# Rebuilding the opening of a hybrid pooling and state-space layer: three projections together over the tiles of x

## The chip, the cores and the metric

The kernel runs on one core of one Trainium2 chip. The metric is the time of one execution on the device, in microseconds (us). All arithmetic is in 32-bit floats; the matmuls use the `float32r` form, and every operand is split into a high part `h` and a rest `l`, so that one product is made of three matmuls (`h*h`, `h*l`, `l*h`).

## The reference

One layer of a streaming encoder, for 384 tokens (256 of a new stream and 8 running streams of 16 each), with a model width of 2048:

```python
def mixer(u, ...):                       # u = rmsnorm(x, g_mix_pre)
    proj = u @ w_in                      # columns: pool 2048 | z 4096 | xBC 6144 | dt 64 | gates 4096
    a_pool, new_pool = pool_mixer(pool_in, ...)   # windows 2,4,8,16, mean minus self, per-group linear map
    ...                                  # causal conv, state-space scan, gated norm -> a_ssd
    merged = gate_A * (a_pool @ w_pool_proj) + gate_B * (a_ssd @ w_ssd_proj)
    return merged @ w_out
x = x + rmsnorm(mixer(...), g_mix_post)
x = x + rmsnorm(square(relu(rmsnorm(x, g_mlp_pre) @ w_up)) @ w_down, g_mlp_post)
```

`rmsnorm` multiplies by one over the root of the mean square of a token. `dt` is a softplus of 64 columns of `proj`, from which decays and running sums for the scan are made.

## The kernel before

Activations lie with channels on partitions: x is 16 tiles of 128 channels by 384 tokens. One projection tile (128 output columns) is 48 matmuls of 128x384: 16 channel tiles times three. Its weights come in two units of 128x1024 (512 KB): `wfetch` issues the DMA on SP's queue into one of three buffers `w`, `wsplit` makes `wh` on ScalarE (L72) and `wl` on VectorE (L74), each with three buffers, and `half` runs the 24 matmuls of a unit (L81 to L83). The gain `g_mix_pre` is folded into x when it is split (`xsplit`, L158 and L159); the norm factor `rstd` is applied after the projections, so that they do not wait for it.

The opening, in the order of the program: the constants `vec` are loaded by GpSimd's queue (the first gains are in them); GpSimd clears a tile `warm`, on which eight matmuls run; the first weight unit (in halves) and x come through SP's queue; projections p0 and p1 run over channel tiles 0 to 7 and then 8 to 15, then p2. The squares of the 16 x tiles (ScalarE, L204) are summed on VectorE (L205), summed over channels by a matmul with ones (`norm_bc`, tile `bc_x`), and the reciprocal root is found by three Newton steps over 128x384 (`rstd`). The tiles of the opening lie in pool `pha`; the next phase's pool `phc` takes their place tile by tile as they come free, and its first tile is `pst`, the pooling state, loaded by GpSimd's queue (L214).

Then come 16 pool tiles. `pool_tile(gi, k4)` reads its projection from PSUM times `rstd` (L230, L231), forms the windows (L246), and leaves the split `dh`, `dl` (L265, L266). After the first tile of group 1, 2 and 3, `pool_map` of the group before runs (tiles `pw`, 48 matmuls). `gate_a(n)` is a projection tile, a product and a sigmoid. After the last group come `gate_a(0)`, `pool_map(3)` and `dt_phase`: a projection of 128 columns, of which 64 are used, a chain of some 30 small operations on VectorE and ScalarE, and 11 transposes on TensorE (tiles `tk`, L345). Then 16 times a gate and a product with `w_pool_proj` (`pp`). A scheduler orders the instructions of each engine at build time; `behind(ins)` puts an instruction behind `ins` in its engine's order. The projections take their PSUM banks from a ring of two (`mmtile`), p0, p1, p2 and the maps from a ring of six (`sstile`).

Of the kernel before, what the change touches and what calls it, by code (L numbers as in the profile page):

```python
# [6 lines left out]
F32 = mybir.dt.float32  # L7
F32R = mybir.dt.float32r
I32 = mybir.dt.int32
# [25 lines left out]
def build(ctx, tc, io):  # L35
# [18 lines left out]
    def sstile(name):  # L54
        return pss.tile([P, 512], F32, tag="ss", name=name)
# [33 lines left out]
    def half(o, q, wl_, rhs):  # L89
        h, l = wl_  # L90
        with behind(last[0] if chain[0] else None):
            for k in range(8):
                i = q * 8 + k
                c = slice(k * P, k * P + P)
                ins = mm3(o, h[:, c], l[:, c], rhs[i][0], rhs[i][1], i == 0, i == len(rhs) - 1)
        last[0] = ins

    def proj(units, rhs, name):
        o = bank[0](f"pj_{name}")[:, :T]
        for q, src in enumerate(units):  # L100
            half(o, q, wload(src, f"{name}_{q}"), rhs)
        return o

    def norm_bc(pool, sumsq, n, name, after=None, out=None):
# [11 lines left out]
        y = pool.tile([P, T], F32, tag="nr", name=f"ny_{name}", bufs=2) if out is None else out  # L116
        v.tensor_scalar(y.bitcast(I32), hm.bitcast(I32), -0.5, MAGIC - 2.0**22 - 2.0**30, ALU.mult, ALU.add)
        for _ in range(3):
            v.tensor_tensor(a, y, y, ALU.mult)
            v.tensor_tensor(a, a, hm, ALU.mult)  # L120
            v.scalar_tensor_tensor(out=y, in0=a, scalar=1.5, in1=y, op0=ALU.add, op1=ALU.mult)
        return y
# [9 lines left out]
    win = io["w_in"]  # L132

    def in_units(i):
        return [win[i, 0], win[i, 1]]

    main = ExitStack()
    small = main.enter_context(tc.tile_pool(name="small", bufs=1, side="right"))
# [4 lines left out]
    pha = ExitStack()  # L143
    pa = pha.enter_context(tc.tile_pool(name="pha", bufs=2, reuse_waits="tile"))

    def xload(lo, hi):
        for k in range(lo, hi):
            x = pa.tile([P, T], F32, name=f"x{k}", bufs=1)
            sy.dma_start(x, io["xT"][k])
            xr.append(x)  # L150

    def xsplit(lo, hi):
        for k in range(lo, hi):
            x = xr[k]
            h = xgp.tile([P, T], F32R, name=f"xgh{k}")
            l = xgp.tile([P, T], F32R, name=f"xgl{k}")
            g1 = vec[:, V_GPRE + k : V_GPRE + k + 1]
            s.activation(h, x, AF.Copy, scale=g1)  # L158
            v.scalar_tensor_tensor(out=l, in0=x, scalar=g1, in1=h.bitcast(F32), op0=ALU.mult, op1=ALU.subtract)  # L159
            xg.append((h, l))  # L160

    gp.dma_start(vec, io["vec"])
    warm = pa.tile([P, 512], mybir.dt.bfloat16, name="warm", bufs=1)
    gp.memset(warm, 0.0)
    gp.memset(onesr.bitcast(F32), 1.0)
    wt = sstile("warm_o")
    for _ in range(NWARM):
        te.matmul(wt, warm[:, :P], warm, start=True, stop=True)
    w = wpool.tile([P, 1024], F32, tag="w", name="w_p0_0")
    h = wpool.tile([P, 1024], F32R, tag="wh", name="wh_p0_0")  # L170
    l = wpool.tile([P, 1024], F32R, tag="wl", name="wl_p0_0")
    for c in (slice(0, 512), slice(512, 1024)):
        sy.dma_start(w[:, c], win[1, 0][:, c])
        xload(len(xr), len(xr) + 4)
        s.activation(h[:, c], w[:, c], AF.Copy)
        v.tensor_tensor(l[:, c], w[:, c], h[:, c].bitcast(F32), ALU.subtract)
    w0 = h, l
    xsplit(0, 8)
    f1 = wfetch(win[2, 0], "p1_0")
    xload(8, 12)  # L180
    f2 = wfetch(win[1, 1], "p0_1")
    xload(12, 16)
    ps = sstile("pj_p0")[:, :T]
    ps1 = sstile("pj_p1")[:, :T]
    early = [ps, ps1]
    xg += [None] * 8
    half(ps, 0, w0, xg)
    half(ps1, 0, wsplit(f1), xg)
    del xg[8:]
    xsplit(8, 12)  # L190
    w2 = wsplit(f2)
    xsplit(12, 16)
    half(ps, 1, w2, xg)
    f3 = wfetch(win[2, 1], "p1_1")
    half(ps1, 1, wsplit(f3), xg)
    sy.dma_start(cst, io["cst"])
    early += [proj(in_units(1 + k), xg, f"p{k}") for k in (2,)]
    acc = pa.tile([P, T], F32, name="acc", bufs=1)
    for k in range(KD):
        if k == 0:  # L200
            s.activation(acc, xr[0], AF.Square)
        else:
            q = pa.tile([P, T], F32, tag="sq", name=f"sq{k}")
            s.activation(q, xr[k], AF.Square)  # L204
            v.tensor_tensor(acc, acc, q, ALU.add)  # L205
    norm_bc(pa, acc, DM, "x", out=rstd)
    pha.close()

    small.tile([P, 56], F32, name="pad_small")
# [2 lines left out]
    with tc.tile_pool(name="phc", bufs=1, reuse_waits="tile") as pc, tc.tile_pool(name="phc2", bufs=2, reuse_waits="tile") as pc2:  # L212
# [7 lines left out]
        A = [None] * KD  # L220
        dd = [[None] * 4 for _ in range(4)]

        def pool_tile(gi, k4):
            w = WINDOWS[gi]
            k = gi * 4 + k4
            ps = early[k] if k < 3 else proj(in_units(1 + k), xg, f"p{k}")
# [39 lines left out]
            v.tensor_tensor(l, d, h.bitcast(F32), ALU.subtract)  # L266
            dd[gi][k4] = (h, l)

        def pool_map(gi):
            for hf in range(2):  # L270
                h, l = wload(io["pool_w"][gi, hf], f"pw{gi}_{hf}")
                for n2 in range(2):
                    n = gi * 4 + hf * 2 + n2
                    o = sstile(f"pw{n}")[:, :T]
                    for k in range(4):
                        c = slice((n2 * 4 + k) * P, (n2 * 4 + k + 1) * P)
                        mm3(o, h[:, c], l[:, c], dd[gi][k][0], dd[gi][k][1], k == 0, k == 3)
                    ah = pc.tile([P, T], F32R, name=f"ah{n}")
                    al = pc.tile([P, T], F32R, name=f"al{n}")
# [5 lines left out]
                    A[n] = (ah, al)  # L285

        def gate_a(n):
            ps = proj(in_units(17 + n), xg, f"ga{n}")
# [4 lines left out]
            return sg  # L293

        def dt_phase(pb):
            ps = proj(in_units(0), xg, "dt")
            n64 = lambda nm: pb.tile([NH, T], F32, name=nm)
            dtb = vec[:NH, V_DTB : V_DTB + 1]
            alog = vec[:NH, V_ALOG : V_ALOG + 1]
            nA = pb.tile([NH, 1], F32, name="nA")  # L300
            s.activation(nA, alog, AF.Exp)
            raw, ab, e, t1, t2, q = (n64(x) for x in ("raw", "ab", "e", "t1", "t2", "q"))
            v.tensor_tensor(raw, ps[:NH], rstd[:NH], ALU.mult)
# [34 lines left out]
            sy.dma_start(decb, dec_scr.partition_broadcast(P))  # L338
            srcs = [cum[:, i * P : i * P + P] for i in range(3)] + [dt[:, i * P : i * P + P] for i in range(3)]
            srcs += [dtw[:, i * P : i * P + P] for i in range(3)] + [nb[:, :P], nb[:, TP:]]  # L340
            for r in range(2):
                part = srcs[r * 8 : r * 8 + 8]
                o = sstile(f"tk{r}")
                for i, a in enumerate(part):
                    te.transpose(o[:, i * NH : i * NH + NH], a, ident[:NH, :NH])  # L345
# [714 lines left out]
```

## Time and profile before

| | us |
|---|---|
| median of 3 runs | 2846.51 (2845.68 to 2846.81) |
| profiled execution, its own time | 2847.36 |
| span of its instructions | 2845.6 |
| TensorE busy in the span | 2818.9 |
| VectorE busy | 1574.4 |
| ScalarE busy | 1096.4 |

The profiled execution's own time is 1.8 us more than its span, which runs from its first to its last instruction. Engines: PE is TensorE (PEld its weight loads), DVE VectorE, ACT ScalarE, POOL GpSimd, SP SyncE; a q behind the name is the engine's queue of instructions. A row of the windows view gives a stretch of the span, its length, the busy time of each engine with its count of instructions, the granted clock of PE, the share of time in which the 16 DMA engines are busy, and GB/s. A row of the timeline gives start, duration, engine, line, operation, tiles and shape, and in brackets the idle time before it and what ended it.

### The profile page before, as it was taken

The page shows a single profiled execution, that of the slowest core. Times are in us where ns is not written, and L with a number is a line of the kernel's source. Part 1 is how long each engine was busy: PE and PEld are TensorE (multiplying, and loading weights), DVE is VectorE, ACT ScalarE, POOL GpSimd, SP SyncE. Part 2 cuts the span into 40 slices and gives each one's busy share as a digit, 9 for nine tenths or more (in the row PEclk, how much of TensorE's full clock was granted, in tenths as well). Part 3 has the DMA queues.
Part 4 walks back from the last instruction along what each step waited for, and adds up shares of the span by engine and source line. Part 5 has one row for each costly group of instructions (what it writes and reads, how often), then busy time and mean ns, then how long its engine had stood idle before and what let it go on. Part 6 is the DMA issues. An engine that isn't in the chain of part 4 may idle for free.

```text
span 2845.6 us, 39445 instructions
## 1 busy us (share of the span) xinstructions
PE 2818.9 (99%) x15823; PEld 2676.3 (94%) x15823; DVE 1574.4 (55%) x2251; ACT 1096.4 (39%) x1592; POOL 97.0 (3%) x156
## 2 busy tenths in 40 slices
PE   8999999999999999999999999999999999999998
PEld 7999999999999999999999987989898998989897
DVE  7674334786887887886533334534444444444445
ACT  5343224444544544444422234533232333333233
POOL 0000000000100100001000000000000000000000
PEclk9999999999999999999999999999999999999999
DMA  5444445556655655656644453333434343343433
GB/s 203 133 133 142 137 137 196 173 184 213 201 181 205 201 181 202 208 199 215 200 154 149 147 181 119 126 127 126 132 126 126 129 131 126 127 130 129 126 127 125
DMA packets 141655, 448.77 MB, mean 158 GB/s; under 512 B 17201, under 2 KB 40817, under 8 KB 136865
## 3 DMA queue, kind: packets, MB, share of 16 engines
q1 hardware_dynamic: 133152, 410.14, 44.5%
q0 software_dynamic: 8320, 36.13, 3.5%
q8 instruction: 124, 2.03, 0.3%
q14 instruction: 59, 0.48, 0.1%
HBM read 404.48 MB, written 41.72 MB: 157 GB/s over the span
## 4 chain that ended last, share of the span: by engine, by line
PE 96%; DVE 2%; ACT 1%; DMA 1%; issue 0%; SPq 0%; DVEq 0%; ACTq 0%
PE pj_up L83 6%; PE pj_up L81 6%; PE pj_up L82 6%; PE wd L775 6%; PE wd L776 6%; PE wd L774 6%; PE pj_x L81 5%; PE pj_x L83 5%; PE pj_x L82 5%; PE pj_sp L82 3%; PE pj_z L81 3%; PE pj_z L82 3%; PE pj_sp L83 3%; PE pj_z L83 3%; PE pj_sp L81 3%; PE pj_pp L83 2%
## 5 line engine op out<-in xcount | busy, mean ns | idle before, releaser
L83 PE MATMUL pj_up<-x1h,wl_up 128*128 128x384 f32 x1024 | 343.1, 335 | 0.4 <-DVE wl_up L74 0.4
L82 PE MATMUL pj_up<-x1l,wh_up 128*128 128x384 f32 x1024 | 343.0, 335 | 0.0
L81 PE MATMUL pj_up<-x1h,wh_up 128*128 128x384 f32 x1024 | 342.9, 335 | 0.0
L74 DVE TENSOR_TENSOR wl_wd<-w_wd,wh_wd 128x1024 fp32r<-128x1024 f32 x127 | 155.6, 1225 | 261.9 <-ACT wh_wd L72 261.9
L775 PE MATMUL wd<-wl_wd,hh 128*128 128x512 f32 x762 | 296.7, 389 | 0.0
L776 PE MATMUL wd<-wh_wd,hl 128*128 128x512 f32 x762 | 296.6, 389 | 0.0
L774 PE MATMUL wd<-wh_wd,hh 128*128 128x512 f32 x762 | 296.2, 389 | 0.0
L72 ACT ACTIVATE wh_wd<-w_wd 128x1024 fp32r<-128x1024 f32 x127 | 134.8, 1061 | 350.7 <-PE wd L776 284.1
L74 DVE TENSOR_TENSOR wl_up<-w_up,wh_up 128x1024 fp32r<-128x1024 f32 x128 | 156.8, 1225 | 199.6 <-ACT wh_up L72 199.6
L72 ACT ACTIVATE wh_up<-w_up 128x1024 fp32r<-128x1024 f32 x128 | 135.8, 1062 | 326.5 <-PE pj_up L82 265.8
L81 PE MATMUL pj_x<-xgh,wh_x 128*128 128x384 f32 x768 | 257.4, 335 | 0.0
L82 PE MATMUL pj_x<-xgl,wh_x 128*128 128x384 f32 x768 | 256.6, 334 | 0.0
L83 PE MATMUL pj_x<-xgh,wl_x 128*128 128x384 f32 x768 | 256.6, 334 | 0.0
L83 PEld LDWEIGHTS pj_up<-x1h,wl_up 128*128 128x128 f32 x1024 | 192.5, 188 | 0.9 <-DVE wl_up L74 0.7
L81 PEld LDWEIGHTS pj_up<-x1h,wh_up 128*128 128x128 f32 x1024 | 192.5, 188 | 0.5
L82 PEld LDWEIGHTS pj_up<-x1l,wh_up 128*128 128x128 f32 x1024 | 192.7, 188 | 0.3
L81 PE MATMUL pj_z<-xgh,wh_z 128*128 128x384 f32 x512 | 171.1, 334 | 0.0
L83 PE MATMUL pj_z<-xgh,wl_z 128*128 128x384 f32 x512 | 171.1, 334 | 0.0
L775 PEld LDWEIGHTS wd<-wl_wd,hh 128*128 128x128 f32 x762 | 143.0, 188 | 29.8 <-DVE wl_wd L74 0.3
L82 PE MATMUL pj_z<-xgl,wh_z 128*128 128x384 f32 x512 | 171.0, 334 | 0.0
L81 PE MATMUL pj_sp<-abh,wh_sp 128*128 128x384 f32 x512 | 171.0, 334 | 0.0
L82 PE MATMUL pj_sp<-abl,wh_sp 128*128 128x384 f32 x512 | 171.0, 334 | 0.0
(292 smaller groups left out, 6089.0 us busy)
## 6 DMA issues: line engine op xcount, KB each, us to landing
w_up<-w_up SPq DMA_DIRECT2D x128, 512.0 KB, 3.4
w_wd<-w_down SPq DMA_DIRECT2D x128, 512.0 KB, 3.4
w_x<-w_in SPq DMA_DIRECT2D x96, 512.0 KB, 4.4
w_z<-w_in SPq DMA_DIRECT2D x64, 512.0 KB, 3.5
w_sp<-w_ssd SPq DMA_DIRECT2D x64, 512.0 KB, 3.5
w_ga<-w_in SPq DMA_DIRECT2D x32, 512.0 KB, 3.4
w_pp<-w_pp SPq DMA_DIRECT2D x32, 512.0 KB, 3.4
hs<-ssm SPq DMA_DIRECT2D x16, 1024.0 KB, 6.4
```

Source lines behind the costliest of these rows:

```text
L72: s.activation(h, w, AF.Copy)
L74: v.tensor_tensor(l, w, h.bitcast(F32), ALU.subtract)
L81: te.matmul(out, wh, xh, start=first, stop=False)
L82: te.matmul(out, wh, xl, start=False, stop=False)
L83: return te.matmul(out, wl, xh, start=False, stop=last)
L774: te.matmul(o[b], mh, wh[:, c], start=k == 0, stop=False)
L775: te.matmul(o[b], mh, wl[:, c], start=False, stop=False)
L776: te.matmul(o[b], ml, wh[:, c], start=False, stop=k == nk - 1)
```

## The change

- The three projections p0, p1 and p2 run together over the channel tiles of x: for each tile k, one strip `w_e[k]` of 128x384 weights, and 9 matmuls. From k = 2 on, strips come in pairs of one DMA of 384 KB.
- All loads of the opening are on SP's queue, in the order of use: x0 with the 16 gains in front of it (`x0g`), strip 0, x1, strip 1, then two x tiles and a pair of strips in turn. `vec` comes last, by the same queue.
- The squares come from x with tokens on partitions (three tiles of 128x2048, 1 MB each, loaded in between), one ScalarE instruction per tile with a running sum; Newton's steps run on 128x3. Three scaled identities, split in two, and two matmuls with ones bring the result into `rstd`.
- p3 belongs to the opening too, in the two-bank ring, ahead of the norm's matmuls.
- `gate_a(0)` moves from before `pool_map(3)` to before `pool_map(0)`, and each `pool_map` in the loop is put behind the last projection on TensorE.
- `dt_phase` comes ahead of `pool_map(3)`. Its 64 columns of high and of low weights are packed side by side into one 128-column operand: two matmuls per channel tile, 32 in all, where there were 48; the upper half is copied down and added. The 11 transposes move behind the gate loop's fourth round (`dt_turn`).

```diff
-    gp.dma_start(vec, io["vec"])
     warm = pa.tile([P, 512], mybir.dt.bfloat16, name="warm", bufs=1)
...
-    for c in (slice(0, 512), slice(512, 1024)):
-        sy.dma_start(w[:, c], win[1, 0][:, c])
-        xload(len(xr), len(xr) + 4)
...
+    x0 = pa.tile([P, KD + T], F32, name="x0g", bufs=1)
+    sy.dma_start(x0, io["x0g"])
...
+    def eload(k, n):
+        w = wpool.tile([P, 1024], F32, tag="w", name=f"w_e{k}")[:, : n * T]
+        sy.dma_start(w.rearrange("p (k n) -> p k n", k=n), io["w_e"][k : k + n].rearrange("k p n -> p k n"))
...
+    eload(0, 1)
+    xload(1)
+    eload(1, 1)
+    for k in range(2, KD, 2):
+        xload(k)
+        xload(k + 1)
+        eload(k, 2)
+        if k in (6, 10):
+            tload(len(xs3))
+    f0 = wfetch(in_units(4)[0], "p3_0")
+    sy.dma_start(ident, io["cst"][:, C_IDENT : C_IDENT + P])
+    tload(2)
+    f1 = wfetch(in_units(4)[1], "p3_1")
+    sy.dma_start(cst[:, P:], io["cst"][:, P:])
+    sy.dma_start(vec, io["vec"])
...
+    for k in range(2, KD, 2):
+        xsplit(k)
+        xsplit(k + 1)
+        hl = esplit(k)
+        eprod(k, 0, hl)
+        eprod(k + 1, 1, hl)
+        if k in (10, 14):
+            square((k - 10) // 4, turn[0])
+    ps3 = mmtile("pj_p3")[:, :T]
+    half(ps3, 0, wsplit(f0), xg)
+    square(2, None)
+    half(ps3, 1, wsplit(f1), xg)
...
+    newton(yx, ax, hx)
+    for b in range(3):
+        y1 = yx[:, b : b + 1]
+        v.tensor_scalar(dgh[:, b, :], ident, y1, None, ALU.mult)
...
+    te.matmul(bc, onesr, dgh.rearrange("p b t -> p (b t)"), start=True, stop=False)
+    te.matmul(bc, onesr, dgl.rearrange("p b t -> p (b t)"), start=False, stop=True)
+    s.copy(rstd, bc)
...
-            ps = proj(in_units(0), xg, "dt")
+            ps = mmtile("pj_dt")[:, :T]
+            for q in range(2):
...
+                for k in range(8):
+                    c = hl[:, k].rearrange("p a n -> p (a n)")
+                    te.matmul(ps, c, xg[q * 8 + k][0], start=q + k == 0, stop=False)
+                    te.matmul(ps, c, xg[q * 8 + k][1], start=False, stop=q * 8 + k == KD - 1)
...
+            with behind(s.copy(raw, ps[NH:])):
+                s.activation(nA, alog, AF.Exp)
+            v.tensor_tensor(raw, ps[:NH], raw, ALU.add)
...
                 if gi and k4 == 0:
-                    pool_map(gi - 1)
-        sg = gate_a(0)
+                    if gi == 1:
+                        sg = gate_a(0)
+                    pool_map(gi - 1, last[0])
+        srcs = dt_phase(pc)
         pool_map(3)
-        dt_phase(pc)
...
+            if n == 3:
+                dt_turn(srcs)
```

More of the change, by code (lines that the diff above doesn't have):

```diff
@@ L102, in proj, with newton, norm_bc @@
         return o
-    def norm_bc(pool, sumsq, n, name, after=None, out=None):
+    def newton(y, a, hm):
+        v.tensor_scalar(y.bitcast(I32), hm.bitcast(I32), -0.5, MAGIC - 2.0**22 - 2.0**30, ALU.mult, ALU.add)
+        for _ in range(3):
+            v.tensor_tensor(a, y, y, ALU.mult)
+            v.tensor_tensor(a, a, hm, ALU.mult)
+            v.scalar_tensor_tensor(out=y, in0=a, scalar=1.5, in1=y, op0=ALU.add, op1=ALU.mult)
+        return y
+    def norm_bc(pool, sumsq, n, name, after=None):
         h = pool.tile([P, T], F32R, tag="nr", name=f"nh_{name}", bufs=2)
@@ L115, in norm_bc @@
         a = pool.tile([P, T], F32, tag="nr", name=f"na_{name}", bufs=2)
[L116 to L122, printed above, removed]
+        y = pool.tile([P, T], F32, tag="nr", name=f"ny_{name}", bufs=2)
+        return newton(y, a, hm)
     a_scr = [dram.tile([P, T], F32, name=f"a_scr{i}") for i in range(32)]
@@ L200, in build, with esplit @@
+    early = [sstile(f"pj_p{n}")[:, :T] for n in range(3)]
+    turn = [None]
+    def esplit(k):
+        w, n = eu[k]
+        h = wpool.tile([P, 1024], F32R, tag="wh", name=f"wh_e{k}")[:, : n * T]
+        l = wpool.tile([P, 1024], F32R, tag="wl", name=f"wl_e{k}")[:, : n * T]
         if k == 0:
-            s.activation(acc, xr[0], AF.Square)
+            v.tensor_copy(h, w)
         else:
-            q = pa.tile([P, T], F32, tag="sq", name=f"sq{k}")
-            s.activation(q, xr[k], AF.Square)
@@ L205, in build, with eprod @@
-            v.tensor_tensor(acc, acc, q, ALU.add)
-    norm_bc(pa, acc, DM, "x", out=rstd)
+            turn[0] = s.activation(h, w, AF.Copy)
+        v.tensor_tensor(l, w, h.bitcast(F32), ALU.subtract)
+        return h, l
+    def eprod(k, j, hl):
+        h, l = hl
+        col = lambda n: slice(j * T + n * P, j * T + n * P + P)
+        xh, xl = xg[k]
+        if k == 0:
+            for a, b in ((h, xh), (h, xl), (l, xh)):
+                for n in range(3):
+                    te.matmul(early[n], a[:, col(n)], b, start=a is h and b is xh, stop=False)
+            return
+        for n in range(3):
+            last[0] = mm3(early[n], h[:, col(n)], l[:, col(n)], xh, xl, False, k == KD - 1)
@@ new lines, in build, with square @@
+    sx, hx, ax, yx = (pa.tile([P, 3], F32, name=f"{n}x", bufs=1) for n in ("s", "h", "a", "y"))
+    def square(b, ins):
+        with behind(ins):
+            s.activation(xs3[b], xs3[b], AF.Square, accum_out=sx[:, b : b + 1])
+    for k in (0, 1):
+        hl = esplit(k) if k == 0 else None
+        xsplit(k)
+        eprod(k, 0, hl or esplit(k))
+    for k in range(2, KD, 2):
+        xsplit(k)
+        xsplit(k + 1)
[4 more added lines that the diff above has]
+            square((k - 10) // 4, turn[0])
@@ L219, in build @@
             bufs.append(b)
-        A = [None] * KD
+        A = [
+            (pc.tile([P, T], F32R, name=f"ah{n}"), pc.tile([P, T], F32R, name=f"al{n}")) for n in range(KD)
+        ]
         dd = [[None] * 4 for _ in range(4)]
@@ L267, in pool_tile, with pool_map @@
             dd[gi][k4] = (h, l)
-        def pool_map(gi):
+        def pool_map(gi, after=None):
             for hf in range(2):
@@ L274, in pool_map @@
                     o = sstile(f"pw{n}")[:, :T]
[L275 to L279, printed above, removed]
+                    with behind(after):
+                        for k in range(4):
+                            c = slice((n2 * 4 + k) * P, (n2 * 4 + k + 1) * P)
+                            mm3(o, h[:, c], l[:, c], dd[gi][k][0], dd[gi][k][1], k == 0, k == 3)
+                    ah, al = A[n]
                     sc = vec[:, V_PSC + n : V_PSC + n + 1]
@@ L987 @@
     w_in = a["w_in"][0]
[L988 removed]
+    cols = [i * P for i in range(3, 16)] + [12352 + i * P for i in range(32)]
     for g in range(G):
```

91 lines of the change are left out of this document (42 added, 49 removed).

## The prediction

> **What bounds the kernel now.** I read the page first, then the windows of 20 us, then TensorE's waits, then the timeline around each hole.
>
> ```profile
> span 2845.6 us, 39445 instructions
> ...
> PE 2818.9 (99%) x15823; PEld 2676.3 (94%) x15823; DVE 1574.4 (55%) x2251; ACT 1096.4 (39%) x1592; POOL 97.0 (3%) x156
> ```
>
> ```profile
> 0.00:20.00 20.00, 14.76 (x63) 10.14 (x64) 12.69 (x21) 15.04 (x27) 1.56 (x7) 1.00 0.92 332
> 20.00:40.00 20.00, 19.31 (x110) 18.76 (x109) 16.48 (x26) 11.11 (x18) 0.77 (x3) 1.00 0.65 213
> 40.00:60.00 20.00, 14.79 (x76) 14.31 (x75) 17.50 (x43) 8.12 (x22) 2.16 (x4) 0.83 0.29 94
> 60.00:80.00 20.00, 20.00 (x118) 20.00 (x117) 12.42 (x21) 9.05 (x16) 1.08 (x2) 1.00 0.42 135
> ```
>
> TensorE is busy for 99% of the span, so elsewhere only fewer matmuls can help. The opening is different: a full stretch holds 118 matmuls, the first three hold 63 (8 of them warm-ups), 110 and 76. The first hole is an early one, the second lies in 40 to 60:
>
> ```profile
> PE pw L81 <- ACT dh L265: 5.2, 1, 5.2
> ...
> PE tk L345 <- DVE cum L319: 0.5, 1, 0.5
> ```
>
> ```profile
> 46.00:48.00 2.00, 0.00 (x0) 0.00 (x0) 2.00 (x6) 1.64 (x8) 0.85 (x2) 0.90 0.39 160
> 48.00:54.00 6.00, 3.19 (x10) 3.03 (x11) 5.94 (x21) 2.62 (x9) 0.77 (x2) 0.50 0.42 125
> 54.00:56.00 2.00, 2.00 (x12) 2.00 (x11) 1.97 (x8) 1.10 (x3) 0.54 (x1) 0.89 0.10 35
> ```
>
> The first pooling map waits 5.2 us for the first pool tiles (VectorE is at 2.00 of 2.00 meanwhile), and that idleness halves the granted clock until about 54.4.
>
> **How much the opening loses.** I count lost time as the time on the clock less the matmuls done at full pitch.
>
> ```profile
> 45.66 0.42 DVE L230 TENSOR_TENSOR pbuf<-pj_p,rstd 128x256 f32<-128x256 f32 x1
> ...
> 50.04 0.17 DVE L262 TENSOR_TENSOR d<-d,pbuf 128x16 f32<-128x16 f32 x1
> ...
> 53.11 0.28 DVE L231 TENSOR_TENSOR pbuf<-pj_p,rstd 128x128 f32<-128x128 f32 x1
> ...
> 77.74 0.42 DVE L230 TENSOR_TENSOR pbuf<-pj_p,rstd 128x256 f32<-128x256 f32 x1 [1.97 <-PE pj_p L83]
> ...
> 86.06 0.42 DVE L230 TENSOR_TENSOR pbuf<-pj_p,rstd 128x256 f32<-128x256 f32 x1 [1.50 <-PE pj_p L83]
> ```
>
> The last two rows are the ends of p5 and p6: 8.32 us for 48 matmuls, a pitch of 0.1733 us. At 77.74 TensorE has done six projections (288), one pooling map (48) and the norm's 2: 338 matmuls, 58.6 us. So 19.1 us are lost by then. The second hole is 5.2 us of waiting and about 1.8 us at half clock (some 3.6 us after the map starts), 7.0 together; 12.1 us are lost ahead of it.
>
> **Part A, the new opening (the large term).** Its start:
>
> ```profile
> 1.26 0.69 POOL L162 DMA_DIRECT2D vec<-vec  x1 [0.82 <-POOLq L1038]
> 1.95 0.54 POOL L164 MEMSET warm<- 128x512 bf16 x1
> ...
> 2.55 3.60 PE L168 MATMUL warm_o<-warm 128*128 128x512 bf16 x8 [2.55 <-POOL warm L164]
> ...
> 6.14 1.63 ACT L158 ACTIVATE xgh<-x,vec 128x384 fp32r<-128x384 f32 x3 [1.98 <-DMA vec<-vec]
> ...
> 6.81 0.45 PE L81 MATMUL pj_p<-xgh,wh_p 128*128 128x384 f32 x1 [0.66 <-ACT xgh L158]
> ```
>
> The first real matmul (6.81) waits for x times its gain, and that for `vec` (6.14). With the gains in x0 this wait goes. What is late next is the warm-up: the memset moves up by the 0.69 us of `vec`'s issue, so the warm matmuls end at about 2.55 + 3.60 - 0.69 = 5.5. I take 5.5 plus 0.4 for matmuls still at a cold clock: 5.9.
>
> Then 144 matmuls, 25.0 us: without stalls the three projections end at 30.9. Splits don't bound it: a pair of channel tiles costs ScalarE two x splits (0.54 each from the row above) and 3/4 of a weight split, VectorE much the same:
>
> ```profile
> L72 ACT ACTIVATE wh_wd<-w_wd 128x1024 fp32r<-128x1024 f32 x127 | 134.8, 1061 | 350.7 <-PE wd L776 284.1 <-PE pj_up L82 66.6
> L74 DVE TENSOR_TENSOR wl_up<-w_up,wh_up 128x1024 fp32r<-128x1024 f32 x128 | 156.8, 1225 | 199.6 <-ACT wh_up L72 199.6
> ```
>
> That is 1.9 us on ScalarE and about 2.0 on VectorE, against 3.1 us of matmuls. The token-major squares add two of about 2.1 us (twice the 1061 ns) to ScalarE; the three-deep rings take those up. The supply may bound it:
>
> ```profile
> 2.00:6.00 4.00, 3.45 (x8) 1.04 (x8) 0.69 (x1) 0.65 (x2) 0.63 (x2) 1.00 0.97 291
> 6.00:12.00 6.00, 4.27 (x20) 3.03 (x19) 4.51 (x9) 5.13 (x11) 0.00 (x0) 1.00 1.01 375
> 12.00:20.00 8.00, 7.03 (x38) 6.07 (x37) 7.48 (x12) 8.00 (x16) 0.00 (x0) 1.00 1.01 397
> 20.00:28.00 8.00, 8.00 (x48) 8.00 (x47) 6.95 (x12) 5.87 (x10) 0.77 (x3) 1.00 0.82 270
> ```
>
> Up to the last pair of strips come 16 x tiles and 16 strips of 192 KB and two token tiles of 1 MB: 8.4 MB. And one load comes that nobody moved:
>
> ```profile
> 20.25 0.54 POOL L214 DMA_DIRECT2D pst<-state_pool  x1 [17.62 <-DMA w_p<-w_in]
> ```
>
> `pst` (0.98 MB) takes the place of the pool's first tiles, up to x4 by their sizes, and was held until x4 had been squared. Now x4's last reader is its split, at about 10 us, so `pst` lands in the middle of the stream: 9.4 MB. At the rates of these rows (291, then 375, then 385 between the last full two) that ends at 2 + 4 + 6 + 15.5 = 27.5. Behind it come the last split, 1.7 us, and the last 18 matmuls, 3.1 us, of which 0.3 can start ahead: 32.0. At 291 GB/s throughout it would be 2 + 32.2 + 4.5 = 38.7; with `pst` outside, 30.9. I take 32.0, nearest to the rows with a full queue: 32.0 - 25.0 = 7.0 us lost, between 5.5 (no stall and no cold matmul) and 13.7.
>
> The Trainium skill bears on this stream ("DMA: Bandwidth & Descriptors", "Rules for kernel authors"): it wants 1 MiB or more per DMA for full bandwidth. The loads here are mostly 192 and 384 KB; the 375 GB/s of 6 to 12, when x tiles of 192 KB were among the loads, speak against a large loss.
>
> Next, p3 runs 8.3 us, to 40.7 with two matmuls of the norm behind it. The norm is ready by then: the third token tile lands some 4 us after the last strips (1.6 MB), its square takes 2.1, eleven operations on 128x3 and six on 128x128 some 4 (0.17 and 0.28 us each, by the rows at 50.04 and 53.11), about 38. Cover left: 2 to 3 us. From 40.7 p4 and `gate_a(0)` give 16.6 us of work ahead of the first map, while the four pool tiles need about 11; so the 5.2 us wait and its half clock go. What is late next is the bank: `gate_a(0)` is the second user after p3 of the two-bank ring, and needs pool tile 3 to have read p3. The rows at 45.66 and 53.11 put that read 7.7 us after the first; with `rstd` at about 41.6 it is done at 49.4, when p4 ends at 49.2. I take 0.4 us, between 0 and 2.
>
> Gain of part A: 19.1 - 7.0 - 0.4 = 11.7 us (between 3.4 and 13.6).
>
> **Part B, dt.** 16 matmuls fewer: 16 x 0.1733 = 2.8 us off TensorE, certain. The moved transposes take with them the 0.5 us wait quoted above. Added: a wait at `pool_map(3)`, which had a gate and now has dt's 32 matmuls as cover.
>
> ```profile
> 177.59 0.42 DVE L230 TENSOR_TENSOR pbuf<-pj_p,rstd 128x256 f32<-128x256 f32 x1 [0.66 <-PE pj_p L83]
> ...
> 184.69 0.56 DVE L266 TENSOR_TENSOR dl<-d,dh 128x384 fp32r<-128x384 f32 x1 [0.59 <-ACT dh L265]
> ```
>
> The last pool tile takes 7.7 us from its projection's end to `dl`. Cover: 32 + 9 matmuls, 7.1 us. That leaves 0.5; the copy of dt's upper half and an exponential may stand ahead of `dh` on ScalarE, so I take 1.0 (0 to 2). All of TensorE's later work is queued behind it. dt's VectorE chain now runs under the map and pp0, and the map's last results have pp0's first 45 matmuls as cover (7.8 us); I cost that at nothing, 1 us if the chain holds them up. Part B: 2.8 + 0.5 - 1.0 = 2.3 us.
>
> **Sum.** 11.7 + 2.3 = 14.0 us off the profiled execution's 2847.36: 2833.4. The median shown is 0.85 lower, so 2832.5. The extra 3 MB of token loads lie in a stage counted above.
>
> **Rivals.**
> 1. *Supply-bound opening.* Short transfers and `pst` hold the stream at 291 GB/s: 13.7 us lost, part A gives 5.0 and the whole 7.3: 2839. For it: the rate of 2 to 6, when 192 KB tiles were the bulk. Against: the next six us.
> 2. *The hole only moves.* The pool tiles still end last at the maps or at `gate_a(0)`'s bank, and about 7 us come back with the halved clock: 2839.5. Against: 16.6 us of cover over 11.
> 3. *Slower: the stream starves.* SP's queue works in order; if it waits for a `w` buffer, x and tokens behind wait too, and the engines run dry between short loads. It costs all of the gain when the 9.4 MB come at below 236 GB/s, and is slower by over 0.2% below about 206 GB/s: at 200 the last strips land at 49, the projections end at 53.5, 28.5 us are lost, and the time is 2854. For it: 20 to 28, when the queue did wait for buffers, ran at 270. Against: the ring of three pairs is refilled well ahead of 3.1 us per pair.
>
> By the skill's rule the third is the one to fear: that page's table has 138 GB/s for a transfer of 64 KB and 341 for 1 MB; no run here shows those. A second rule, "TensorE: Matmul & The Clock Gate", Part 1, says that an idle window of 3.4 us throttles the clock; the trace has it after some 2 us (idle from about 45.6, clock at 0.90 in 46 to 48). By the trace a stall of 2 us in the stream could already add 1.8 us; the range has it.
>
> **How the numbers follow.** Forecast 0.66, rival 1 0.14, rival 2 0.08, rival 3 0.06; 0.06 for smaller losses together that bring it within 0.2% (5.7 us, about what a measurement of this kernel can tell). The upper end 2839.5 takes in rivals 1 and 2; the lower 2829.5 is no stall at all: 13.6 + 2.8 + 0.5 = 16.9. Faster 0.88, same 0.06, slower 0.06.
>
> **What would show it.** First real matmul near 5.5; the three projections' end near 32; no wait of `pw` for `dh`; no 0.50 clock at 48 to 54; `pst` issued near 10 us; `pj_dt` with 32 matmuls; a short wait of `pw` behind dt. DMA rates below 300 GB/s between 6 and 27, or a wait of several us at `pj_ga`, would prove me wrong.

## The result, and the profile after

The changed kernel takes 2836.1 us (median of 6 runs, 2834.49 to 2838.28), the kernel before 2846.66 beside it (6 runs, 2845.68 to 2847.43): 10.6 us or 0.37% less, a ratio of 0.9963 [0.995, 0.9976]. 2832.5 was forecast, within 2829.5 to 2839.5. The profiled execution of the changed kernel took 2834.49, with a span of 2832.7: 12.9 less than the span before.

The head of its page, then TensorE's waits in the first 700 us (what waited for what: us in total, times, longest), then the windows of 20 us:

```profile
span 2832.7 us, 39399 instructions
...
PE 2812.7 (99%) x15807; PEld 2673.1 (94%) x15807; DVE 1562.9 (55%) x2245; ACT 1092.0 (39%) x1582; POOL 96.6 (3%) x155
```

```profile
PE pj_ga L81 <- DVE pbuf L291: 3.5, 1, 3.5
PE warm_o L154 <- POOL warm L150: 1.3, 1, 1.3
PE pj_p L81 <- ACT wh_e L212: 0.4, 1, 0.4
```

```profile
0.00:20.00 20.00, 18.28 (x86) 15.41 (x87) 11.61 (x19) 12.38 (x20) 0.87 (x6) 1.00 0.92 335
20.00:40.00 20.00, 20.00 (x117) 20.00 (x116) 12.76 (x29) 13.84 (x17) 0.84 (x3) 1.00 0.92 367
40.00:60.00 20.00, 16.55 (x96) 16.26 (x95) 17.16 (x45) 9.51 (x26) 2.72 (x5) 1.00 0.49 150
60.00:80.00 20.00, 20.00 (x118) 20.00 (x117) 10.77 (x15) 10.16 (x15) 0.54 (x1) 1.00 0.40 132
```

TensorE's matmuls in the first three stretches rise from 63, 110 and 76 to 86, 117 and 96. The waits of `pw` and of `tk` are gone, and 40 to 60 is at full clock. One hole is left: `gate_a(0)` waits 3.5 us for VectorE to read pool tile 3 out of its bank. The timeline around it, of TensorE, VectorE and ScalarE in turn:

```profile
52.14 0.41 PE L81 MATMUL pj_ga<-xgh,wh_ga 128*128 128x384 f32 x1 [3.45 <-DVE pbuf L291]
```

```profile
40.90 0.42 DVE L290 TENSOR_TENSOR pbuf<-pj_p,rstd 128x256 f32<-128x256 f32 x1 [0.36 <-ACT rstd L264]
...
41.97 1.21 DVE L74 TENSOR_TENSOR wl_ga<-w_ga,wh_ga 128x1024 fp32r<-128x1024 f32 x1
45.53 1.23 DVE L74 TENSOR_TENSOR wl_ga<-w_ga,wh_ga 128x1024 fp32r<-128x1024 f32 x1 [2.35 <-ACT wh_ga L72]
46.67 1.30 DVE L306 TENSOR_TENSOR win<-pbuf 128x518 f32<-128x518 f32 x2
...
51.71 0.28 DVE L291 TENSOR_TENSOR pbuf<-pj_p,rstd 128x128 f32<-128x128 f32 x1
```

```profile
42.12 0.30 ACT L300 COPY pstg<-pbuf 128x120 f32<-128x120 f32 x1
44.44 1.06 ACT L72 ACTIVATE wh_ga<-w_ga 128x1024 fp32r<-128x1024 f32 x1 [2.01 <-PE pj_p L82]
45.40 0.47 ACT L297 COPY pbuf<-pst 128x120 f32<-128x120 f32 x2
...
48.55 1.06 ACT L72 ACTIVATE wh_pw<-w_pw 128x1024 fp32r<-128x1024 f32 x1 [0.25 <-PE pj_p L82]
```

The pool tiles start at 40.9 (41.6 was forecast), and tile 3's read ends at 52.0, 11.1 us after, not 7.7. In the middle both engines stand still. ScalarE has the second weight split of `gate_a(0)` next in its order, and that waits 2.0 us for a `wh` buffer, which p4's matmuls hold. Behind it stand two small copies from `pst` (L297) which the pool tiles need; VectorE waits 2.35 us at its own half of the same split, with the window sums (L306) behind it.

The first matmul of the next large phase (`pj_x`) marks the end of everything that the change touches: it starts at 462.23 before and at 450.14 after, 12.1 us earlier. I use that time below. The remaining 0.8 of the two spans lies behind it, where the two programs do the same work.

### The profile page after: what moved, and what is told of

It reads as the page before. It is cut to its first block, busy times and chain, and to the rows that moved or that the text cites. A ratio compares the mean times of both kernels' runs of the same rounds, so it can differ in the third digit from the quotient of the medians.

```text
span 2832.7 us, 39399 instructions
## 1 busy us (share of the span) xinstructions
PE 2812.7 (99%) x15807; PEld 2673.1 (94%) x15807; DVE 1562.9 (55%) x2245; ACT 1092.0 (39%) x1582; POOL 96.6 (3%) x155
## 4 chain that ended last, share of the span: by engine, by line
PE 98%; DVE 1%; ACT 0%; DMA 0%; issue 0%; SPq 0%; DVEq 0%; ACTq 0%
PE pj_up L83 6%; PE pj_up L81 6%; PE pj_up L82 6%; PE wd L853 6%; PE wd L854 6%; PE wd L852 6%; PE pj_x L81 5%; PE pj_x L83 5%; PE pj_x L82 5%; PE pj_sp L82 3%; PE pj_z L81 3%; PE pj_z L82 3%; PE pj_sp L83 3%; PE pj_z L83 3%; PE pj_sp L81 3%; PE pj_ga L81 2%
## 5 line engine op out<-in xcount | busy, mean ns | idle before, releaser
L854 PEld LDWEIGHTS wd<-wh_wd,hl 128*128 128x128 f32 x762 | 143.0, 188 | 29.7
```

Of the source, the lines that this page charges most:

```text
L854: te.matmul(o[b], ml, wh[:, c], start=False, stop=k == nk - 1)
```

## The experiments

"The opening's mark" is the start of that first `pj_x` matmul in the profiled execution. The kernel before ran beside all of them, at medians of 2846.55 to 2846.74.

**1. The changed kernel again**, as the base for the others.

> The changed kernel itself, on the same chip as the next three. Theory (clock gate): its spread comes from the 3.5 us hole ahead of gate_a(0), which is as long as the gate's window of 3.4 us and costs a stretch of half clock in some executions and none in others; so some executions lie near 2834.5 and others 1.5 to 4 us above, and the profiled one has either no 0.50 stretch near 50 us (time near 2834.5) or one (near 2836 to 2838). Rival (chip noise): the spread is of every kernel here, and kernels without the hole show it too.

Median 2837.16 (5 runs, 2835.14 to 2838.86), ratio 0.9967 [0.9954, 0.9979]. The profiled execution has the same hole of 3.5 us, but a span of 2836.3 and the mark at 453.04, 2.9 later. The windows of 2 us, first of the changed kernel's first profile and then of this one, tell why (the columns are those of the other windows; the granted clock is the third number from the end):

```profile
50.00:52.00 2.00, 0.00 (x0) 0.00 (x0) 2.00 (x6) 0.94 (x6) 0.54 (x1) 1.00 0.00 0
52.00:54.00 2.00, 1.86 (x11) 1.89 (x12) 2.00 (x6) 1.06 (x4) 0.54 (x1) 1.00 0.20 69
```

```profile
50.00:52.00 2.00, 0.00 (x0) 0.00 (x0) 2.00 (x6) 0.94 (x6) 0.54 (x1) 0.89 0.01 2
52.00:54.00 2.00, 1.79 (x6) 1.82 (x7) 2.00 (x7) 1.06 (x4) 0.54 (x1) 0.50 0.19 67
```

The same hole was followed by a halved clock (until 58.4) in one execution and not in the other. So a hole of this length has two prices, 3.5 us and about 6.4; the difference is of the size of this kernel's scatter, 3.7 us. The granted clock over each run goes the same way: 0.998 in the fastest of the five (2835.14), 0.996 in the two slowest (2838.12 and 2838.86). The rival holds in part: the kernel before scatters by 2.5 us, and the next kernel, which lacks the hole, by 2.3.

**2. p3 in the ring of six**, so that `gate_a(0)` needs no bank that p3 holds.

```diff
-    ps3 = mmtile("pj_p3")[:, :T]
+    ps3 = sstile("pj_p3")[:, :T]
```

> p3 takes its PSUM bank from the ring of six instead of the ring of two, so gate_a(0) need not wait for pool tile 3 to read it. Theory (the hole is the bank): the 3.5 us wait of pj_ga goes to 0 to 0.3, nothing else on TensorE waits for it because the first map needs dl of tile 3 only 18 us after p4's start; span 3.5 us shorter than the changed kernel's 2832.7, near 2829.2, median near 2831, and all runs within 1 us of each other since no hole over 2 us is left. Rival (the hole moves): the pool tiles still end last and pw waits 2 to 4 us for dl; time within 1 us of the changed kernel. Rival (noise): median falls by 3.5 but the spread of 4 us stays.

Median 2831.46 (5 runs, 2830.39 to 2832.68), ratio 0.9947 [0.9933, 0.9961]. No wait is left behind the opening; TensorE's waits and two of the windows:

```profile
PE pj_p L81 <- ACT wh_e L212: 1.4, 1, 1.4
PE warm_o L154 <- POOL warm L150: 1.3, 1, 1.3
```

```profile
40.00:60.00 20.00, 20.00 (x117) 20.00 (x116) 17.24 (x41) 10.92 (x28) 2.71 (x5) 1.00 0.48 161
60.00:80.00 20.00, 20.00 (x117) 20.00 (x116) 12.77 (x25) 10.23 (x16) 0.54 (x1) 1.00 0.44 149
```

The mark is at 447.05, 3.1 earlier than the best of the changed kernel (the hole's 3.5, less 1.0 more at the start, where the wait for a strip differs from run to run; the 0.6 left I did not place). This kernel (kernel 2 below) has the lowest median of all: 5.7 us below the changed kernel on the same chip, and none of its runs reaches into that one's. The runs were to lie within 1 us of each other; they spread over 2.3, all at a granted clock of 0.998, so part of the scatter has another cause, which stays open.

**3. One split moved behind the pool tiles.** If the waiting split causes the hole, its place in the order should matter. The second split of `gate_a(0)` goes behind tile 3's read and copy (`read3`, on VectorE and ScalarE; `hold` puts the next split behind them); the bank stays in the ring of two.

```diff
+                hold[:] = read3
+                half(ps, 1, wload(u[1], "ga0_1"), xg)
+                hold[:] = [None, None]
```

> The bank stays in the ring of two; only the order changes: the split of gate_a(0)'s second weight unit (wh on ScalarE, wl on VectorE) is put behind pool tile 3's read of p3. Theory (queue order): in the changed kernel ScalarE's copies of the pooling state stand behind that wh, which waits 2.0 us for a weight buffer, and VectorE's window sums behind both; with the split behind, tile 3 reads p3 at about 48.5 instead of 52.0, the wait of pj_ga falls from 3.5 to about 0.4 us, and the time is within 1 us of the kernel with six banks. Rival (VectorE is simply full): the reads come no earlier than 51, the wait stays at 3 us or more, or turns into a wait of pj_ga for its second unit.

Median 2835.45 (5 runs, 2834.85 to 2836.53), ratio 0.9961 [0.9949, 0.9974]. The expectation missed: 2.9 us of the hole stayed. The three engines again (the first row names a small operation on `d`, which stands next to tile 3's read; the read, L292, ends at 52.35, 0.15 us before the matmul, as in the changed kernel):

```profile
52.50 0.47 PE L81 MATMUL pj_ga<-xgh,wh_ga 128*128 128x384 f32 x1 [2.89 <-DVE d L325]
```

```profile
46.76 0.41 DVE L291 TENSOR_TENSOR pbuf<-pj_p,rstd 128x256 f32<-128x256 f32 x1
...
50.97 0.56 DVE L329 TENSOR_TENSOR dl<-d,dh 128x384 fp32r<-128x384 f32 x1 [2.10 <-ACT dh L328]
...
52.07 0.28 DVE L292 TENSOR_TENSOR pbuf<-pj_p,rstd 128x128 f32<-128x128 f32 x1
```

```profile
49.47 1.06 ACT L72 ACTIVATE wh_pw<-w_pw 128x1024 fp32r<-128x1024 f32 x1 [2.26 <-PE pj_p L82]
50.43 0.51 ACT L328 ACTIVATE dh<-d 128x384 fp32r<-128x384 f32 x1
```

Tile 2 was read 2.5 us earlier (46.76 against 49.22). Then the next split in the order, `wh_pw` of the map, took the place of the first: it waits 2.26 us for a buffer, `dh` stands behind it, `dl` waits for `dh`, and tile 3's read stands behind `dl`.

**4. Both splits behind.** As 3, and the map's first split behind the last `dh` of group 0 (`split[3]`) as well.

```diff
+                if gi == 0 and hf == 0:
+                    hold[:] = [split[3], read3[1]]
                 h, l = wload(io["pool_w"][gi, hf], f"pw{gi}_{hf}")
+                hold[:] = [None, None]
```

> As the kernel with the gate's second split behind pool tile 3's read, and the first pooling map's weight split (wh_pw, which stood next in ScalarE's queue and waited 2.3 us there for a buffer) behind the last dh of group 0 as well; the bank stays in the ring of two. Theory (ScalarE's queue: a weight split that waits for a buffer holds up the small copies and dh behind it, and VectorE behind those): tile 3 reads p3 near 50.3 instead of 52.1, the wait of pj_ga falls from 2.9 to 1.0 to 1.5 us. Rival (VectorE's own work is what is late): the read stays at 51.5 or later and the wait at 2.5 us or more.

Median 2832.95 (4 runs, 2832.25 to 2833.69), ratio 0.9954 [0.9937, 0.997]; the mark is at 447.83, and the clock stays full. Tile 3's read ends at 49.7.

```profile
PE pj_ga L81 <- DVE d L325: 1.0, 1, 1.0
```

With the bank still in the ring of two, the order of two splits alone cuts the hole from 3.5 to 1.0. So the cause has two halves, either of which can be taken away: a bank that must be read first, and a reader that stands behind waiting splits.

**5. The order alone, without the new opening.** The kernel before, with `gate_a(0)` ahead of the first map, the maps behind the last projection, dt ahead of `pool_map(3)` and the transposes later.

```diff
-                    pool_map(gi - 1)
-        sg = gate_a(0)
+                    if gi == 1:
+                        sg = gate_a(0)
+                    pool_map(gi - 1, last[0])
+        srcs = dt_phase(pc)
         pool_map(3)
-        dt_phase(pc)
```

> The kernel before, with its old opening and its 48 matmuls for dt, and only the order changed: gate_a(0) before pool_map(0), maps behind the last projection, dt ahead of pool_map(3), transposes behind the fourth round of the gate loop. Theory (the second hole is a matter of order): of the 7.0 us of the hole at 46 to 54 most goes; p3's bank is read at about 53.4, when p4 ends, so the wait is under 1 us, the 0.5 us of tk goes too: 6.5 to 7.5 us faster than before, near 2839.5. Theory (the rebuild of the loads does the work): under 3 us faster, with a hole of 3 us or more at pj_ga.

Median 2847.35 (11 runs, 2846.54 to 2850.64), ratio 1.0004 [0.9995, 1.0013]: nothing gained. The hole went to a place that I had not named, the start of p4. In the windows of 2 us before it TensorE does nothing, and the clock halves:

```profile
PE pj_p L81 <- DVE pbuf L231: 6.2, 1, 6.2
```

```profile
46.00:48.00 2.00, 0.00 (x0) 0.00 (x0) 2.00 (x4) 1.28 (x8) 1.08 (x2) 1.00 0.21 77
48.00:50.00 2.00, 0.00 (x0) 0.00 (x0) 2.00 (x9) 0.72 (x3) 0.00 (x0) 0.55 0.62 148
50.00:52.00 2.00, 0.58 (x2) 0.61 (x3) 1.94 (x8) 1.41 (x5) 0.00 (x0) 0.50 0.45 160
```

I had missed that p2 too has its bank in the ring of two: the description of the kernel before puts it into the ring of six, and that is wrong (only p0, p1 and the maps are there). p4 needs p2's bank, and p2 is read only once the norm is there. In the kernel before, the same bank was taken until the second row here ends, at 51.64:

```profile
50.81 1.01 PE L81 MATMUL pw<-dh,wh_pw 128*128 128x384 f32 x2 [5.21 <-ACT dh L265]
```

```profile
51.36 0.28 DVE L231 TENSOR_TENSOR pbuf<-pj_p,rstd 128x128 f32<-128x128 f32 x1
```

Three of the map's matmuls stood ahead of p4 in TensorE's order, and p4 began right behind them, at 51.94. So the old hole had two causes that ended within 1 us of each other, `dh` for the map and p2's bank for p4, and taking away the first alone gains nothing.

**6. The order and the banks, without the new opening.** As 5, with p2 and p3 both made early and in the ring of six.

```diff
+    bank[0] = sstile
+    early += [proj(in_units(1 + k), xg, f"p{k}") for k in (2, 3)]
+    bank[0] = mmtile
```

> The kernel before with its old opening, its loads, its norm and its 48 matmuls for dt; the new order (gate_a(0) ahead of pool_map(0), dt ahead of pool_map(3), transposes late), and p2 and p3 in the ring of six, since with order alone the 6.2 us wait stood at p4 for p2's bank. Theory (the second hole is order and banks, the opening's rebuild isn't needed for it): no wait over 1 us between 40 and 70, the 7.0 us of the hole and 0.5 of tk go; the first matmul of pj_x starts near 455 instead of 462.2, and the time is near 2839.5. Rival (the norm has to come earlier too): a wait of 3 us or more at pj_p, pj_ga or pw stays, and the time is above 2843.

Median 2840.72 (10 runs, 2839.51 to 2841.28), ratio 0.9979 [0.997, 0.9988]; the mark is at 456.35. About 2839.5 and a mark near 455 were expected, with no wait over 1 us. With banks to go with it, the order alone brings 5.9 us at the mark, half of what the whole change did, at full clock and with a rest of 1.4 us before the first map:

```profile
PE pw L81 <- ACT dh L267: 1.4, 1, 1.4
```

**7. dt with 48 matmuls again**, on kernel 2.

```diff
-            ps = mmtile("pj_dt")[:, :T]
...
+            ps = proj([io["w_in"][125, 0], io["w_in"][125, 1]], xg, "dt")
```

> The changed kernel with p3 in the ring of six (no hole left at the gate), and dt's projection as before: 48 matmuls with the full unit pair of 128 columns in place of the packed 32. Theory (TensorE's count is all that counts there): 16 x 0.1733 = 2.8 us slower than the six-bank kernel's 2831.5, near 2834.2, and the first matmul of pj_x 2.8 us later than its 447.05 (less or more by the early stall, which was 1.4 us in that profile). Rival (hidden, or the packing costs as much as it saves in the chain behind it): within 1 us of the six-bank kernel.

Median 2833.32 (4 runs, 2833.04 to 2833.67), ratio 0.9954 [0.9939, 0.9969]. The mark is at 449.83, 2.8 after kernel 2's, which fits the 16 matmuls of the packing; but TensorE's early waits for strips differ between the two profiles (0.9 here, 1.4 there), so the 2.8 is good to about half a us. The median moved by only 1.9, on another chip.

**8. The norm from channel-major x**, on kernel 2: `norm_x` makes 16 squares and their sum, splits it, runs two matmuls with ones between the halves of p3, and takes Newton's steps on 128x384; no token loads.

```diff
-        if k in (6, 10):
-            tload(len(xs3))
...
+    norm_x()
     half(ps3, 1, wsplit(f1), xg)
```

> The changed kernel with p3 in the ring of six, and the norm as before: squares of the 16 channel tiles, summed on VectorE, two matmuls between the halves of p3, Newton's steps on 128x384; no token-major loads (3 MB less in the opening's stream). Theory A (the token-major norm carries part of the gain): rstd is ready near 44.5 instead of 41, the pool tiles end 3 to 4 us later, pw or pj_ga waits 2 to 3 us, and the time is 2 to 4 us above the six-bank kernel's 2831.5. Theory B (p4 and the gate give cover enough, the norm's form is worth nothing): within 1 us of it, or a little faster since the early stall for the strips goes with the 3 MB.

Median 2835.79 (4 runs, 2832.37 to 2837.12), ratio 0.9961 [0.9946, 0.9976]. The profiled execution was the fastest of these, with the mark at 447.69 and a wait of 0.7 us at `bc_x`, in the middle of p3; it does not explain the others. A second profile of the same kernel:

> The kernel with the channel-major norm and p3 in the ring of six once more, for a second profile: its first profile had no wait over 0.7 us in the opening and a time near 2832.4, while its other executions lay between 2835.7 and 2837.1. Theory (a late rstd leaves the pool tiles so little room that a slightly later stream opens a wait at pw): this profile shows a wait of pw or pj_p of 1 us or more between 40 and 70 us, or a 0.50 stretch of the clock there, and a time above 2834. Rival (the difference lies elsewhere): no wait over 1 us before 450 us, and the loss shows further on, or the time is near 2832.4 again.

This execution took 2835.82, with the mark at 450.63. The first matmul of the norm, and two windows behind it:

```profile
37.48 0.41 PE L255 MATMUL bc_x<-nh_x,onesr 128*128 128x384 f32 x1 [1.85 <-ACT nh_x L252]
```

```profile
38.00:40.00 2.00, 2.00 (x10) 2.00 (x11) 1.55 (x2) 0.28 (x1) 0.00 (x0) 0.82 0.58 234
40.00:42.00 2.00, 2.00 (x8) 2.00 (x7) 1.90 (x5) 0.00 (x0) 0.00 (x0) 0.50 0.35 63
```

The sum of squares from channels comes later than TensorE wants it, by 0.7 us in one execution and 1.85 in the other, and the longer wait also brought a halved clock. Neither theory had this place: the wait stands at the norm's own matmul, and no wait of `pw` or `pj_ga` follows. Over the runs the granted clock is 0.998 in the fast one and 0.997 in the other three and in the second profile. The kernel with the token-major norm is about 4 us faster in the median (2835.79 against 2831.46, on two chips); what was run against it is the old norm with its matmuls inside p3, and the old norm with them behind p3 was not run. Two profiles are not enough to explain every run.

**9. `pst` early**, on kernel 2: `x0g` is allocated behind the other x tiles, so that it no longer lies where `pst` goes.

```diff
+    xt_ = {k: pa.tile([P, T], F32, name=f"x{k}", bufs=1) for k in range(1, KD)}
     x0 = pa.tile([P, KD + T], F32, name="x0g", bufs=1)
```

> The changed kernel with p3 in the ring of six, and one change of layout: x0 with the gains lies behind x15 in the opening's pool, so that pst (0.98 MB, GpSimd's queue) takes the place of x1 to x5 and can go out once x5 is split, near 11 us, instead of 27.3 us, where the last read of the gains held it. This is the state that the prediction assumed. Theory (the stream has slack for it): the strips land 2.5 us later, TensorE waits 0 to 0.5 us more, the time is within 0.5 us of the six-bank kernel's 2831.5. Theory of the prediction (supply binds): the three projections end 1 to 2 us later, pj_p waits for wh_e or xgl between 15 and 30 us, the time is 1 to 2 us longer.

GpSimd's issue of `pst`, first in the changed kernel and then here, and TensorE's waits here:

```profile
27.33 0.68 POOL L272 DMA_DIRECT2D pst<-state_pool  x1 [25.92 <-DMA cst<-cst]
```

```profile
12.15 0.68 POOL L273 DMA_DIRECT2D pst<-state_pool  x1 [10.75 <-DMA w_e<-w_e]
```

```profile
PE pj_p L81 <- ACT wh_e L213: 3.5, 4, 1.5
```

Median 2834.05 (4 runs, 2832.56 to 2834.99), ratio 0.9956 [0.9942, 0.9969], and the mark at 449.79, 2.7 us later than kernel 2's. With 0.98 MB more in the stream, strips come late: behind `pst` TensorE waits 1.27 us until 20.46 and 1.54 until 28.54, where kernel 2 has no wait (its 1.4 ends at 10.08).

**10. Strips 2 and 3 as loads of their own**, on kernel 2, since the first pair is what TensorE waits for at 10 us.

```diff
-    for k in range(2, KD, 2):
+    for k in (2, 3):
+        xload(k)
+        eload(k, 1)
+    for k in range(4, KD, 2):
```

> The six-bank kernel, and strips 2 and 3 as loads of their own behind their x tiles, in place of one pair; the only wait left in its opening is TensorE's for the split of that first pair (0.4 us in one profile, 1.4 in another). Theory (the first pair comes late because it waits for its second half and a 768-wide split): that wait goes, 0.4 to 1.2 us off the six-bank kernel's 2831.5, near 2830.7. Rival (the stream itself is late there): the wait moves to the next strip and the time stays within 0.3 us.

Median 2832.83 (5 runs, 2831.05 to 2833.94), ratio 0.9952 [0.9938, 0.9965], the mark at 448.22; not better. The waits now stand at the following strips:

```profile
PE pj_p L81 <- ACT wh_e L215: 1.5, 3, 0.8
...
PE pj_p L83 <- DVE wl_e L216: 0.4, 1, 0.4
```

**11. The new opening with `gate_a(0)` at its old place**, behind the last group; p3 stays in the ring of two.

```diff
-                    if gi == 1:
-                        sg = gate_a(0)
                     pool_map(gi - 1, last[0])
+        sg = gate_a(0)
         srcs = dt_phase(pc)
```

> The complement of order and banks alone: the changed kernel (p3 in the ring of two, its loads, its norm, packed dt), but gate_a(0) back behind the last pool tile, as before the change. Theory (the gate is the cover of the pool tiles): pw stands right behind p4, which ends near 48.3, and waits for dh and dl of the group, which come between 50 and 57: a hole of 5 to 7 us with half clock behind it; the first matmul of pj_x 3 to 5 us later than the changed kernel's 450.1, and the time near 2840. Rival (the earlier norm is enough): wait under 3 us, time within 1 us of the changed kernel's 2836 to 2837.

Median 2833.8 (4 runs, 2833.42 to 2833.99), ratio 0.9955 [0.9941, 0.9969]; the mark is at 448.61.

```profile
PE pw L81 <- ACT dh L325: 1.4, 1, 1.4
...
PE pj_ga L81 <- ACT wh_ga L72: 0.6, 1, 0.6
```

I had expected the old hole of `pw` to return. It is 1.4 us. The norm comes some 5 us earlier here than in the kernel before, and the whole map still stands behind p4, which keeps TensorE busy until 48.4; the map then starts at 49.83 on tiles 0 and 1 while tiles 2 and 3 are being made. The move of `gate_a(0)`, by itself, thus costs the changed kernel time (no run of this kernel reaches those of the changed one, 2833.99 against 2834.49 at the nearest): it put the gate on a bank that was not free.

## Why the prediction was right, and where it was not

**Start and stream: right in the sum, wrong in its parts.** The first real matmul starts at 4.35 (5.5 was said: the warm-up's memset moved up by 1.2 us, not by the 0.69 of one issue, so the warm matmuls end at 4.9). The 0.4 for matmuls at a cold clock had no row behind it, and it was too small:

```profile
4.35 1.52 PE L223 MATMUL pj_p<-xgh,wh_e 128*128 128x384 f32 x3
5.67 0.93 PE L223 MATMUL pj_p<-xgl,wh_e 128*128 128x384 f32 x3
6.43 0.69 PE L223 MATMUL pj_p<-xgh,wl_e 128*128 128x384 f32 x3
6.96 0.38 PE L81 MATMUL pj_p<-xgh,wh_e 128*128 128x384 f32 x1
```

The nine matmuls of the first three rows take 2.6 us, up to the start of the fourth row, where full pitch is 1.6. From 5.03 to 5.99 they start 0.32 us apart, the same distance as in the half-clock stretch of experiment 1's profile (52.67, 52.99, 53.31), and from 6.26 on 0.17; the record of the granted clock begins only at 6.2. So that term is 1.0.

p3's first matmul, the end of the three projections, is at 31.5 against 32.0. Time lost by then is 31.5 - 25.0 = 6.5 us, 7.0 forecast, of which 1.1 stood for the stream. Another 1.1 was indeed lost after the first nine matmuls, but before 12 us and not at the step that I gave: 0.4 is the wait for the first pair of strips, the rest lies in smaller gaps around strips 1 and 2. That the two agree is luck. `pst` was to land in the middle of the stream, since x4's last reader is its split; but it also lies over `x0g`, whose gains every split reads, and was issued at 27.3, when the last strips had landed. Experiment 9 shows the step's price when it does happen: 2.7 us, not the 1.1 between 30.9 and 32.0. From 20 us on the transfers ran faster than the 385 GB/s that I took:

```profile
6.00:8.00 2.00, 1.97 (x10) 1.60 (x10) 1.57 (x3) 1.94 (x4) 0.00 (x0) 1.00 0.97 351
...
20.00:28.00 8.00, 8.00 (x48) 8.00 (x47) 5.20 (x8) 6.99 (x10) 0.67 (x1) 1.00 1.05 407
28.00:38.00 10.00, 10.00 (x60) 10.00 (x59) 5.69 (x20) 5.79 (x7) 0.17 (x3) 1.00 0.98 402
```

So rivals 1 and 3 are out: the stream stays at 351 GB/s and more from 6 to 38 us, and TensorE waits for no strip longer than 0.4 us in this profile (1.4 in that of kernel 2).

**The norm and the map's hole: right, with a part that was luck.** p3 and the norm's matmuls end at 40, `rstd` is read at 40.9 and the 5.2 us wait of `pw` with its halved clock is gone. The prediction saw only `dh` behind that wait. Experiment 5 shows p2's bank there too, at 6.2 us; the change removes it because it takes p2 into the ring of six, which I had believed to be so already.

**The bank: the step that failed.** The term was 0.4 us, between 0 and 2 (by its own figures p4 ends at 40.7 + 8.3 = 49.0, not 49.2, and the read at 49.3; the term hardly changes). It measured 3.45, outside its own range; where the clock halves it is about 6.4. The mechanism was named rightly, down to the wait at `pj_ga`. Its size came from the 7.7 us between two reads in the trace of before. There, nothing of `gate_a(0)` stood in the engines' orders among the pool tiles: VectorE had one weight split between those two reads, the map's (1.22 us), and did not wait for it. The change puts that gate's two splits there instead. On VectorE the second one brings 2.35 us of waiting and 1.23 of work, with small pool operations behind it; these 3.6 us are about the difference between 7.7 and 11.1. I counted the moved step's matmuls as cover and its bank as a wait, but not its splits on ScalarE and VectorE. Experiments 2 and 4 show both halves, and experiment 3 that moving one split is not enough. This is also what became of rival 2: part of the hole did move, to `gate_a(0)`, at 3.5 us rather than 7.

By the end of p5, with 386 matmuls done (66.9 us), the changed kernel has lost 10.5 us:

```profile
77.41 0.42 DVE L290 TENSOR_TENSOR pbuf<-pj_p,rstd 128x256 f32<-128x256 f32 x1 [2.02 <-PE pj_p L83]
```

Part A is therefore 19.1 - 10.5 = 8.6 us, where 11.7 was said. Of the 3.1 missing, the bank's excess is 3.05; the 0.5 that start and stream did better is lost again between p3 and p5, in places that I did not find.

**dt: right, and a little low.** From p15's end to the last matmul of the map, 80 matmuls, pass 14.1 us against 13.9 at full pitch: the wait at `pool_map(3)` that I took as 1.0 is 0.25. The 16 matmuls are worth 2.8, which experiment 7 fits, and `tk` waits no more. Part B is 12.1 - 8.6 = 3.5 us at the mark (2.3 forecast), of which I can place 2.8 + 0.5 - 0.25 = 3.05.

**The sum.** 12.1 us at the mark and 12.9 over the span, against 14.0. The profiled execution was the fastest of six, one without the halved clock; the median lies 1.6 above it, and the second profile shows 2.9 at the mark for that clock. The prediction had a price for such a stall (1.8 us), but kept it in the range and not in the number.

**What each part is worth**, at the mark, from profiles of the changed kernels without a halved clock there (the kernel before has one): order and banks on the old opening 5.9; the new opening, dt and late transposes without the gate's move 13.6 (experiment 11); the whole change 12.1; with the bank as well 15.2. The parts overlap, since both remove the same hole ahead of the first map. Each figure is one profile, and the wait for the first strips alone differs by 1.0 us between profiles.

## What to carry to other kernels

When a step is moved up to cover a wait, move all of it in your mind: its matmuls are the cover, but its bank and its weight splits are new users of rings, and in an engine that works in order, a split that waits for a buffer (2.0 us here) holds every small operation behind it. Count the users of a PSUM ring between a tile's start and its last read; here one word, another ring, was worth 5.7 us in the median, more than half of what the large change brought. A load into reused memory starts at the last reader of whatever lies there, which may be a table of gains and not the tile that one has in mind.

## What was not expected of the hardware

The price of a short hole is not fixed. Waits of 3.45 us (the changed kernel) cost a halved clock of 6.8 us in one execution and none in another; 2.9 us (experiment 3) cost 3.4 us of it; 1.85 us (experiment 8, second profile) 3.4 us; 1.0 to 1.5 (experiments 2, 4, 6, 9 and 11) none in the profiles here. The stretches at half clock in the middle of the runs last 3.41 or 6.83 us, one or two units of the same length. The Trainium skill ("TensorE: Matmul & The Clock Gate", Part 1, "What's actually happening") describes a free-running window of 3413 ns; the lengths agree with that, and a free-running window would make the price depend on where in it the hole falls.

The kept traces bear this out in part. In each profile the full-clock stretches between two drops are whole multiples of that unit too (in experiment 1's profile 1703.25 us from 58.38 to 1761.63, 499 units), so all changes of the clock in an execution lie on one grid, and the grid starts at another place in each execution. In experiment 1's profile 2.8 us of the hole lie in the unit from 48.14 to 51.55, at whose end the clock drops. In the changed kernel's first profile (reckoned back 500 units from its drop at 1757.23) a boundary at 50.56 cuts the hole into 1.9 and 1.6 us, and there is no drop. It is not the whole rule: in experiment 8's second profile 1.7 idle us within one unit were enough, where 1.9 were not in the changed kernel's first. The same section of the Trainium skill also asks for one idle window of that length; here 1.7 to 2.9 us of one were followed by a drop, and there the measurement decides. No run here sets the place of the grid, so that it decides between the two prices is argued from these few executions.
